# Memory keys of a decoder layer: the 512-column matmuls of a tile first, the 256-column ones behind them, and the weight rests held behind the addition that frees the bank

## The chip, the cores and the metric

The kernel runs on one core of a Trainium2 chip. The metric is the device time of one execution in microseconds (us). Before the change it is 844.3 us, the median of 3 runs (843.54 to 844.47). The profile and the trace come from one more execution of the same kernel, which took 844.19 us.

## The reference, cut to what matters

One decoder layer is computed: a mixer (stick-breaking attention and a short convolution), a cross-attention into 256 memory tokens, a SwiGLU block and a last norm. The change touches one product of the cross-attention, the memory keys.

```python
def memory_cross_attention(h, m, w_q, w_kv, w_o):
    q = (h @ w_q).reshape(b, s, MEM_HEADS, MEM_HEAD_DIM)
    kv = (m @ w_kv).reshape(b, mlen, 2, MEM_HEADS, MEM_HEAD_DIM)
    k, v = kv[:, :, 0], kv[:, :, 1]
    scores = jnp.einsum('bshd,bmhd->bhsm', q.astype(jnp.float32), k.astype(jnp.float32))
```

Here m is the normed memory, 256 x 1024, and the keys k are m times the first 1024 columns of w_kv.

## The kernel before

All products are made in fp32r in pieces: an f32 operand is split into a rounded part (hi) and the rest that the rounding left (lo), and hi x hi, hi x lo and lo x hi are added up. Weights come in tiles of 128 x 1024 through `load_w` (lines 139 to 153): SyncE starts a DMA into `wr`, ScalarE rounds it into `wh` (line 151, "the cast"), and VectorE subtracts to get `wl` (line 152, "the weight rest"). Each of `wr`, `wh` and `wl` has four buffers, so a load, a cast and a rest can run up to four tiles ahead of the matmuls that read them, and a buffer is free again when the matmuls of four tiles before are through.

The memory is held transposed, in 8 blocks of 128 of the 1024 features. For each block k, `mgs[k]` holds 512 columns: 256 memory tokens rounded (that is `mg[k][0]`) and 256 rests. The keys are made in 8 output tiles m of 128 key columns (lines 656 to 676). For one tile, the loop over k issues two matmuls each: one with `wh` over all 512 columns of `mgs[k]` (line 661), which gives hi x hi in the left half of the bank and hi x lo in the right half, and one with `wl` over the 256 rounded columns (line 663), which adds lo x hi to the left half. Then

```python
        t = tmp("km", MEM)
        nc.scalar.copy(t, ps[:, MEM:])
        nc.vector.tensor_tensor(out=t, in0=ps[:, :MEM], in1=t, op=ALU.add)
        nc.vector.tensor_tensor(out=t, in0=t, in1=rmb, op=ALU.mult)
```

ScalarE copies the right half out (line 666, "the copy"), VectorE adds the left half to it (line 667, "the addition", the last reader of the bank), multiplies by the tokens' norm factor (line 668) and, after ScalarE's rounding of the result (line 672), subtracts for the key's own rest (line 673). The banks come from a pool of two (`pmm`), so the first matmul of tile m waits for the addition of tile m-2.

Ahead of the keys stands the loop over the 8 tiles of the merged branches (`br`); behind them stand the memory values, 8 weight tiles with 12 matmuls of 512 columns each (`vm`, lines 677 to 690). The order of the instructions on each engine in this part is set by the scheduler of the framework, from the order in the code, the dependencies, and extra order-only dependencies that `after(i, earlier)` adds (line 107): i is then placed behind the instructions in `earlier`. `lows` (line 104) collects the weight rests of all `load_w` calls.

Of the kernel before, what the change touches and what calls it, by code (L numbers as in the profile page):

```python
# [11 lines left out]
ALU = mybir.AluOpType  # L12
# [4 lines left out]
KD = D // P  # L17
# [4 lines left out]
MEM = 256  # L22
# [22 lines left out]
def hybrid_layer(ctx: ExitStack, tc: tile.TileContext, xT_d, memT_d, mem_d, cols_d, wv_d, win_d,  # L45
                 wbr_d, wmix_d, wmq_d, wmk_d, wmv_d, wmo_d, wfi_d, wfo_d, gfin_d, out):
    nc = tc.nc
# [16 lines left out]
    def nm(s):  # L64
        count[0] += 1
        return f"{s}{count[0]}"

    def unit(s, cols=512):
        return upool.tile([P, cols], F32R, tag="u", name=nm(s), padded_shape=[P, 512])

    def tmp(s, cols=512):
        return tpool.tile([P, cols], F32, tag="t", name=nm(s), padded_shape=[P, 512])

    def f(ap):
        return ap.bitcast(F32)

    def mmtile(s, pool=None, tag="mm"):
        return (pool or pmm).tile([P, 512], F32, tag=tag, name=nm(s))

    def ztile(s):  # L80
        return mmtile(s, pz, "z")
# [22 lines left out]
    exps, casts, lead, lows, loads = [], [], [], [], []  # L104
    HALVES = slice(0, HD), slice(HD, P)

    def after(i, earlier):
        for e in earlier:
            tc.add_manual_dep(i.ins, e.ins.name, mybir.DependencyInfo(
                mybir.DependencyClass.NoSync, mybir.DependencyReason.DATA), reason="order")  # L110
# [23 lines left out]
    def chained(i):  # L134

        after(i, chain[-1:])
        chain.append(i)

    def load_w(src, cols=P):

        k = D // cols
        raw = wpool.tile([P, D], F32, tag="wr", name=nm("wr"))
        i = nc.sync.dma_start(raw, src)
        loads.append(i)
        if count[1] < FIRST:
            count[1] += 1
            chained(i)
        hi = wpool.tile([P, k, cols], F32R, tag="wh", name=nm("wh"))
        lo = wpool.tile([P, k, cols], F32R, tag="wl", name=nm("wl"))
        h2, l2 = (t.rearrange("p k c -> p (k c)") for t in (hi, lo))  # L150
        after(nc.scalar.copy(h2, raw), lead[-1:])  # L151
        lows.append(nc.vector.tensor_tensor(out=l2, in0=raw, in1=f(h2), op=ALU.subtract))  # L152
        return hi, lo

    def mm3(ps, a, b, start, stop, **kw):
        nc.tensor.matmul(ps, a[0], b[0], start=start, stop=False, **kw)  # L156
        nc.tensor.matmul(ps, a[0], b[1], start=False, stop=False, **kw)  # L157
        nc.tensor.matmul(ps, a[1], b[0], start=False, stop=stop, **kw)  # L158
# [11 lines left out]
    def split(src, s, scale=None, cols=512, last=()):  # L170

        hi, lo = unit(s + "h", cols), unit(s + "l", cols)
        if scale is None:
            casts.append(nc.scalar.copy(hi, src))
            after(casts[-1], last)
            nc.vector.tensor_tensor(out=lo, in0=src, in1=f(hi), op=ALU.subtract)
        else:
            nc.scalar.activation(hi, src, AF.Copy, scale=scale)
            nc.vector.scalar_tensor_tensor(out=lo, in0=src, scalar=scale, in1=f(hi),
                                           op0=ALU.mult, op1=ALU.subtract)  # L180
        return hi, lo
# [449 lines left out]
    for m in range(KD):  # L631
        sig = []
        for j in range(2):
            if (m, j) not in gates:
                gate(m, j)
            t = gates.pop((m, j))
# [4 lines left out]
        for j in (1, 0):  # L641
            if m == 0 and j == 0:
                gate(EARLY, 0)
            ps = mmtile("br")
# [8 lines left out]
            mem_split(m)  # L653


    km = []
    for m in range(KD):
        w = load_w(wmk_d[m])
        ps = mmtile("km")
        for k in range(KD):  # L660
            nc.tensor.matmul(ps, w[0][:, k, :], mgs[k], start=k == 0, stop=False,
                             skip_group_check=True)
            nc.tensor.matmul(ps[:, :MEM], w[1][:, k, :], mg[k][0], start=False, stop=k == KD - 1,
                             skip_group_check=True)
        t = tmp("km", MEM)
        nc.scalar.copy(t, ps[:, MEM:])
        nc.vector.tensor_tensor(out=t, in0=ps[:, :MEM], in1=t, op=ALU.add)
        nc.vector.tensor_tensor(out=t, in0=t, in1=rmb, op=ALU.mult)
        if m % 2 == 0:
            pair = unit("kmh"), unit("kml")  # L670
        hi, lo = (u[:, (m % 2) * MEM:(m % 2 + 1) * MEM] for u in pair)
        nc.scalar.copy(hi, t)
        nc.vector.tensor_tensor(out=lo, in0=t, in1=f(hi), op=ALU.subtract)
        km.append((hi, lo))
        if m == 0:
            merged.append(split(sig[0], "m"))
    vm = [[None] * 2 for _ in range(MT)]
    for n in range(2):
        pss = [ztile("vm") for _ in range(MT)]
        for c in range(4):  # L680
            w = load_w(wmv_d[n, c], 512)
            for j in range(2):
                k = 2 * c + j
                for t in range(MT):
                    sl = slice(t * P, (t + 1) * P)
                    mm3(pss[t], (mg[k][0][:, sl], mg[k][1][:, sl]),
                        (w[0][:, j, :], w[1][:, j, :]), k == 0, k == KD - 1)
        for t in range(MT):
            vm[t][n] = split(pss[t], "vm", rm[:, t:t + 1])
# [81 lines left out]
    for h in range(MH):  # L771
        q = q_next
        scs = []
        for t2 in range(2):
            ps = ztile("sc")
            scs.append(ps)
            for i in range(2):
                t = 2 * t2 + i
# [5 lines left out]
        for t2 in range(2):  # L784
            ps = scs[t2]
# [5 lines left out]
                                           in1=r1s[:, 2 * t2:2 * t2 + 2], op0=ALU.mult,  # L791
# [3 lines left out]
            for i in range(2):  # L795
                t = 2 * t2 + i
# [5 lines left out]
            for i in range(2):  # L802
                nc.vector.tensor_scalar(out=pr[:, i * MEM:(i + 1) * MEM],
                                        in0=pr[:, i * MEM:(i + 1) * MEM],
# [5 lines left out]
        for t in range(TT):  # L810
            for m in range(MT):
                c = (t % 2) * MEM + m * P
                nc.tensor.transpose(pt[m][:, t * P:(t + 1) * P], prs[t // 2][:, c:c + P], ident)
        ptr = [split(pt[m], "pt") for m in range(MT)]
        for j in range(2):
            ps = ztile("om")
            c = h * 256 + j * P
# [261 lines left out]
    with tc.manual_schedule(engines={mybir.EngineType.PE, mybir.EngineType.Activation,  # L1079
# [97 lines left out]
        for j in range(2, NJ - 2):  # L1177
# [6 lines left out]
            if NJ - 2 - LIGHT <= j + 1 < NJ - 2 + 1:  # L1184
                n = j + 1 - (NJ - 2 - LIGHT)
# [273 lines left out]
```

## Time and profile before

| what | value |
|---|---|
| time of the runs shown, median (lowest, highest) | 844.3 us (843.54, 844.47) |
| the profiled execution's own time | 844.19 us |
| its span | 842.4 us |
| TensorE busy / VectorE / ScalarE / GpSimd | 833.8 / 658.7 / 464.2 / 155.6 us |
| stretch of the memory keys, first key matmul to first of the values proper | 300.39 to 324.19 us |

The span is the time from the first to the last instruction of the profiled execution; 1.8 us of its time lie outside. A row of the timeline has the start and the duration in us, the engine, the line, the operation and its tiles. Matmuls are pipelined: the duration of one is from its start to its modelled end, and the next one starts before that, so what a matmul costs TensorE is the step from its start to the next start, not its duration. PE is TensorE's matmuls, PEld its weight loads, ACT ScalarE, DVE VectorE, POOL GpSimd and SP SyncE.

### The profile page before, as it was taken

How to read it: one execution, taken by the hardware profiler on the slowest of the kernel's cores; microseconds unless marked ns; L12 is line 12 of the kernel's file. 1: busy time of each engine (PE TensorE's matmuls, PEld its weight loads, DVE VectorE, ACT ScalarE, POOL GpSimd, SP SyncE). 2: the span in 40 equal slices, each digit the busy share in tenths (PEclk: the TensorE clock that was granted, in tenths of full speed). 3: DMA queues.
4: the chain of work that ended last, by engine and by line, in shares of the span. 5: the costliest groups of instructions: out<-in, count | busy, mean ns of one | idle time of the engine just before them, and what ended most of it. 6: DMA issues, size and time to landing. Idle time of an engine off the chain costs nothing.

```text
span 842.4 us, 12559 instructions
## 1 busy us (share of the span) xinstructions
PE 833.8 (99%) x4694; PEld 731.0 (87%) x4694; DVE 658.7 (78%) x1066; ACT 464.2 (55%) x835; POOL 155.6 (18%) x165
## 2 busy tenths in 40 slices
PE   9999999999999999999999999999999999999996
PEld 7888888888888888888888889999999999988885
DVE  7879899986756577586555679888887888899886
ACT  7567878674332255433444557655555555666654
POOL 0011131210666620173000101111111110000401
PEclk9999999999999999999999999999999999999998
DMA  8452454134687865566431425777677772465552
GB/s 301 151 168 102 120 115 114 59 116 172 244 308 269 315 231 189 187 230 238 134 80 51 113 51 153 198 184 190 178 181 194 189 181 85 150 224 202 176 186 101
DMA packets 51359, 143.73 MB, mean 171 GB/s; under 512 B 5761, under 2 KB 7041, under 8 KB 48482
## 3 DMA queue, kind: packets, MB, share of 16 engines
q1 hardware_dynamic: 41650, 107.89, 38.5%
q0 software_dynamic: 9360, 34.75, 15.8%
q8 instruction: 37, 0.61, 0.3%
q10 hardware_dynamic: 288, 0.28, 0.1%
q14 instruction: 24, 0.20, 0.1%
HBM read 125.20 MB, written 13.64 MB: 165 GB/s over the span
## 4 chain that ended last, share of the span: by engine, by line
PE 98%; DMA 1%; DVE 0%; ACT 0%; issue 0%; SPq 0%; DVEq 0%
PE z L883 15%; PE p L1152 12%; PE pr L156 8%; PE pr L157 8%; PE pr L158 8%; PE y L883 8%; PE v L883 4%; PE r L157 3%; PE r L156 3%; PE r L158 3%; PE v L284 2%; PE mq L157 2%; PE mq L158 2%; PE mq L156 2%; PE br L157 2%; PE br L156 2%
## 5 line engine op out<-in xcount | busy, mean ns | idle before, releaser
L151 ACT CAST wh<-wr 128x1024 fp32r<-128x1024 f32 x84 | 88.1, 1051 | 149.4 <-issue 83.7
L152 DVE TENSOR_TENSOR wl<-wr,wh 128x1024 fp32r<-128x1024 f32 x84 | 112.2, 1336 | 37.2 <-ACT wh L151 37.2
L156 PE MATMUL pr<-xgh,wh 128*128 128x512 f32 x288 | 112.8, 392 | 0.0
L157 PE MATMUL pr<-xgl,wh 128*128 128x512 f32 x288 | 112.3, 390 | 0.0
L158 PE MATMUL pr<-xgh,wl 128*128 128x512 f32 x288 | 112.2, 390 | 0.0
L607 POOL TENSOR_TENSOR pre<-pre 128x512 f32<-128x512 f32 x44 | 70.1, 1597 | 32.6 <-DMA pre<-in_w_ffn_out_dram 30.3
L852 POOL DMA_DIRECT2D ws<-in_w_ffn_in_dram x22 | 26.6, 1210 | 256.2 <-DVE wf L873 123.5
L883 PE MATMUL z<-xdh,wf 128*128 128x256 f32 x352 | 70.4, 283 | 0.0
L158 PEld LDWEIGHTS pr<-xgh,wl 128*128 128x128 f32 x288 | 54.1, 188 | 11.6
L156 PEld LDWEIGHTS pr<-xgh,wh 128*128 128x128 f32 x288 | 54.1, 188 | 10.6
L157 PEld LDWEIGHTS pr<-xgl,wh 128*128 128x128 f32 x288 | 54.1, 188 | 10.3
L904 ACT COPY sa<-z 128x256 f32<-128x256 f32 x44 | 16.4, 372 | 81.5 <-PE z L883 81.5
L883 PEld LDWEIGHTS z<-xdh,wf 128*128 128x128 f32 x352 | 58.0, 192 | 0.0
L873 DVE TENSOR_TENSOR wf<-s,wf 128x512 fp32r<-128x512 f32 x44 | 30.4, 690 | 25.7 <-ACT wf L872 25.3
L883 PE MATMUL z<-xdl,wf 128*128 128x256 f32 x176 | 49.8, 283 | 0.0
L964 DVE TENSOR_TENSOR wl<-wr,wh 128x1024 fp32r<-128x1024 f32 x33 | 41.0, 1242 | 4.3 <-ACT wh L1031 4.3
L1031 ACT CAST wh<-wr 128x1024 fp32r<-128x1024 f32 x33 | 34.6, 1050 | 4.4 <-DMA wr<-sums 2.1
L883 PE MATMUL y<-xch,wf 128*128 128x256 f32 x176 | 35.4, 283 | 0.0
L883 PE MATMUL v<-xoh,wf 128*128 128x256 f32 x176 | 35.4, 283 | 0.0
L883 PE MATMUL z<-xf,wf 128*128 128x256 f32 x264 | 35.4, 283 | 0.0
L883 PE MATMUL z<-xch,wf 128*128 128x256 f32 x176 | 35.3, 283 | 0.0
L883 PE MATMUL y<-xoh,wf 128*128 128x256 f32 x176 | 35.3, 283 | 0.0
(350 smaller groups left out, 2377.5 us busy)
## 6 DMA issues: line engine op xcount, KB each, us to landing
wr<-in_w_in_dram SPq DMA_DIRECT2D x36, 512.0 KB, 3.3
pre<-in_w_ffn_out_dram POOLq DMA_DIRECT2D x11, 1024.0 KB, 7.9
sums<-pre POOLq DMA_DIRECT2D x11, 1024.0 KB, 5.1
ws<-in_w_ffn_in_dram SPq DMA_DIRECT2D x22, 512.0 KB, 3.7
wg<-in_w_ffn_in_dram SPq DMA_DIRECT2D x22, 512.0 KB, 4.5
ws<-in_w_ffn_in_dram POOLq DMA_DIRECT2D x22, 512.0 KB, 6.1
wr<-sums SPq DMA_DIRECT2D x22, 512.0 KB, 3.9
wr<-in_w_ffn_out_dram SPq DMA_DIRECT2D x16, 512.0 KB, 3.9
```

The lines of the kernel that those rows point to most:

```text
L151: after(nc.scalar.copy(h2, raw), lead[-1:])
L152: lows.append(nc.vector.tensor_tensor(out=l2, in0=raw, in1=f(h2), op=ALU.subtract))
L156: nc.tensor.matmul(ps, a[0], b[0], start=start, stop=False, **kw)
L157: nc.tensor.matmul(ps, a[0], b[1], start=False, stop=False, **kw)
L158: nc.tensor.matmul(ps, a[1], b[0], start=False, stop=stop, **kw)
L607: nc.gpsimd.tensor_tensor(out=t[:, a, :], in0=t[:, a, :], in1=t[:, b, :], op=ALU.add)
L852: nc.gpsimd.dma_start(s13, a[:, 0:4:3, :], accum_op=ALU.add)
L873: nc.vector.tensor_tensor(out=w[:, 1, :], in0=raw, in1=f(w[:, 0, :]), op=ALU.subtract)
L883: nc.tensor.matmul(ps[:, :HS], a, b, start=i < 3 and k == 0 and j == 0, stop=k == KP - 1 and j == 2, skip_group_check=True)
L964: nc.vector.tensor_tensor(out=lo, in0=src, in1=f(hi), op=ALU.subtract)
L1031: nc.scalar.copy(hi, raw)
L1152: nc.tensor.matmul(res[i][s2], a[:, ts], b, start=j == 0 and n == 0, stop=n == 2 and j == (BEHIND - 1 if (i, s2) == (5, 1) else NJ - 1))
```

## The change

Three things change. In a key tile, the loop over k is split in two: first the 8 matmuls of 512 columns with `wh`, then the 8 of 256 columns with `wl`. The additions of the 8 tiles are collected in `ready`. And a weight rest is ordered behind an addition: that of key tile m behind the addition of tile m-4 (for m above 3), and those of the first four tiles of the memory values behind the additions of key tiles 4 to 7.

```diff
-    km = []
+    km, ready = [], []
     for m in range(KD):
         w = load_w(wmk_d[m])
+        after(lows[-1], ready[m - 4:m - 3] if m > 3 else ())
         ps = mmtile("km")
         for k in range(KD):
             nc.tensor.matmul(ps, w[0][:, k, :], mgs[k], start=k == 0, stop=False,
                              skip_group_check=True)
+        for k in range(KD):
             nc.tensor.matmul(ps[:, :MEM], w[1][:, k, :], mg[k][0], start=False, stop=k == KD - 1,
                              skip_group_check=True)
         t = tmp("km", MEM)
         nc.scalar.copy(t, ps[:, MEM:])
-        nc.vector.tensor_tensor(out=t, in0=ps[:, :MEM], in1=t, op=ALU.add)
+        ready.append(nc.vector.tensor_tensor(out=t, in0=ps[:, :MEM], in1=t, op=ALU.add))
...
         for c in range(4):
             w = load_w(wmv_d[n, c], 512)
+            if n == 0:
+                after(lows[-1], ready[c + 4:c + 5])
```

TensorE's order changes in every key tile. The rows are those at the end of key tile 1 (bank `km_2964`, weights `wh_2960` and `wl_2961`) and the start of tile 2 (bank `km_2993`). Before, TensorE has:

```order
L661 MATMUL km_2964<-mg_2378,wh_2960 128x512
L663 MATMUL km_2964<-mg_2378,wl_2961 128x256
L661 MATMUL km_2964<-mg_2381,wh_2960 128x512
L663 MATMUL km_2964<-mg_2381,wl_2961 128x256
L661 MATMUL km_2964<-mg_2493,wh_2960 128x512
L663 MATMUL km_2964<-mg_2493,wl_2961 128x256
L661 MATMUL km_2964<-mg_2496,wh_2960 128x512
L663 MATMUL km_2964<-mg_2496,wl_2961 128x256
L661 MATMUL km_2993<-mg_2181,wh_2989 128x512
```

With the change, TensorE has at the same place:

```order
L662 MATMUL km_2964<-mg_2493,wh_2960 128x512
L662 MATMUL km_2964<-mg_2496,wh_2960 128x512
L665 MATMUL km_2964<-mg_2181,wl_2961 128x256
L665 MATMUL km_2964<-mg_2184,wl_2961 128x256
L665 MATMUL km_2964<-mg_2296,wl_2961 128x256
L665 MATMUL km_2964<-mg_2299,wl_2961 128x256
L665 MATMUL km_2964<-mg_2378,wl_2961 128x256
L665 MATMUL km_2964<-mg_2381,wl_2961 128x256
L665 MATMUL km_2964<-mg_2493,wl_2961 128x256
L665 MATMUL km_2964<-mg_2496,wl_2961 128x256
L662 MATMUL km_2993<-mg_2181,wh_2989 128x512
```

The last reader of `wh_2960` stands 8 matmuls ahead of the tile's end now, where it stood one ahead. One matmul of the values (`vm_3167` with `wh_3171`), which stood between key tiles 5 and 6, stands behind tile 7 now.

VectorE's order changes around each addition. In this piece of the difference the names `km_2946` and `km_2981` are the results of key tiles 0 and 1, `kml_2951` their own rests, and `wl_3021`, `wl_3050` and `wl_3081` the weight rests of key tiles 3, 4 and 5; the rows with + are those of the change.

```order
 L152 TENSOR_TENSOR wl_3021<-wr_3018,wh_3020 128x1024
+L669 TENSOR_TENSOR km_2946<-km_2929,km_2946 128x256
 L152 TENSOR_TENSOR wl_3050<-wr_3047,wh_3049 128x1024
-L667 TENSOR_TENSOR km_2946<-km_2929,km_2946 128x256
-L668 TENSOR_TENSOR km_2946<-km_2946,rmb 128x256
+L670 TENSOR_TENSOR km_2946<-km_2946,rmb 128x256
+L675 TENSOR_TENSOR kml_2951<-km_2946,kmh_2950 128x256
+L669 TENSOR_TENSOR km_2981<-km_2964,km_2981 128x256
 L152 TENSOR_TENSOR wl_3081<-wr_3078,wh_3080 128x1024
-L673 TENSOR_TENSOR kml_2951<-km_2946,kmh_2950 128x256
-L667 TENSOR_TENSOR km_2981<-km_2964,km_2981 128x256
 L176 TENSOR_TENSOR ml_2955<-g_2851,mh_2954 128x512
```

The addition of tile 1 (lines 667 and 669) stood behind the weight rest of tile 5 and stands ahead of it now; so it is with the other tiles. ScalarE keeps its order but for one cast (`wh_3253`) that stands one place later, and SyncE and GpSimd keep theirs.

## The prediction

> **What bounds the kernel now.** The page comes first, for the engine that fills the span.
>
> ```profile
> span 842.4 us, 12559 instructions
> PE 833.8 (99%) x4694; PEld 731.0 (87%) x4694; DVE 658.7 (78%) x1066; ACT 464.2 (55%) x835; POOL 155.6 (18%) x165
> ```
>
> TensorE is busy for 99% of the span, so the time can only fall where its matmuls come closer together. The profiled execution took 844.19 us, 1.8 us more than its span and 0.1 us less than the median of the runs shown (844.3). Busy time hides short waits here, since a matmul's record is longer than its step. So I read next the timeline of TensorE in the stage of the keys, by the starts.
>
> ```profile
> 297.67 0.39 PE L156 MATMUL br<-oh,wh 128*128 128x512 f32 x1
> ...
> 300.39 0.39 PE L661 MATMUL km<-mg,wh 128*128 128x512 f32 x1
> 300.62 0.28 PE L663 MATMUL km<-mg,wl 128*128 128x256 f32 x1
> 300.73 0.40 PE L661 MATMUL km<-mg,wh 128*128 128x512 f32 x1
> ...
> 303.20 0.40 PE L661 MATMUL km<-mg,wh 128*128 128x512 f32 x1
> ...
> 305.68 0.40 PE L661 MATMUL km<-mg,wh 128*128 128x512 f32 x1
> 305.92 0.28 PE L663 MATMUL km<-mg,wl 128*128 128x256 f32 x1
> 306.03 0.49 PE L661 MATMUL km<-mg,wh 128*128 128x512 f32 x1
> 306.36 0.28 PE L663 MATMUL km<-mg,wl 128*128 128x256 f32 x1
> ...
> 308.79 0.28 PE L663 MATMUL km<-mg,wl 128*128 128x256 f32 x1
> 309.19 0.50 PE L661 MATMUL km<-mg,wh 128*128 128x512 f32 x1
> 309.53 0.27 PE L663 MATMUL km<-mg,wl 128*128 128x256 f32 x1
> ...
> 318.15 0.40 PE L156 MATMUL vm<-wh,mg 128*128 128x512 f32 x1
> 318.38 0.40 PE L661 MATMUL km<-mg,wh 128*128 128x512 f32 x1
> ...
> 324.19 0.39 PE L157 MATMUL vm<-wl,mg 128*128 128x512 f32 x1
> ```
>
> From 297.67 to 300.39 twelve matmuls of 512 columns start, 0.2267 us each: that is the step where nothing waits. The key tiles then take from 300.39 to 324.19, 23.80 us, of which 0.23 belong to the one matmul of the values at 318.15; 23.57 us are the keys' own. The first tile takes 2.81 us (300.39 to 303.20), 0.351 for a pair of a long and a short matmul. At the start of tile 3 the short matmul at 308.79 is followed only after 0.40 us, and the next long one takes a step of 0.34 (309.19 to 309.53). At the start of tile 2 it is 0.33 (306.03 to 306.36). The chain of waits, for the same stretch, says who came late.
>
> ```profile
> 306.16 1.06 ACT wh L151
> 307.25 1.22 DVE wl L152
> 308.47 0.34 DVE kml L673
> 308.81 0.35 DVE km L667
> 309.19 0.50 PE km L661
> ```
>
> Tile 3 needs the bank of tile 1. Tile 1's last long matmul ends at 306.08 (305.68 + 0.40); 0.08 later ScalarE casts the weights of tile 5, VectorE makes their rest, then the rest of key tile 0, and only then the addition that frees the bank. That is 3.1 us from matmul to matmul, where TensorE has one short matmul and one tile to fill it. The view of waits puts the sum at 1.1 us in three waits; the others are spread over long first steps.
>
> ```profile
> PEld km L661 <- DVE km L667: 1.1, 3, 0.4
> ```
>
> **The change part by part.** It adds and removes no instruction; it moves matmuls, rests and additions.
>
> *The long matmuls first.* The stage has 64 steps of 512 columns and 64 of 256. The long step is 0.2267 us, from above. For the short step in a row of its like the feed-forward stage has a row of the chain:
>
> ```profile
> 680.63 4.32 PE z L883 x36
> ```
>
> 36 matmuls of 256 columns in 4.32 us are 0.120 us each. In the key stage itself a short one between two long ones has a step of 0.11 (300.62 to 300.73), and its weight load lasts 0.188:
>
> ```profile
> L663 PEld LDWEIGHTS km<-mg,wl x64: 187/188/190, 300.4 to 323.8; 128*128 128x128 f32 x64
> ```
>
> So the short step is unknown between 0.11 and 0.188; I take 0.120, since the 36 have the same shape, fp32r and a new weight each. A tile is then 8 x (0.2267 + 0.120) = 2.773 us, and eight are 22.19 us if nothing waits. Against the 0.351 of a pair in the first tile, the new order saves 0.004 a pair, some 0.29 us in the stage if all tiles were like the first; the rest of the gain is the waits.
>
> *Does the bank come free in time?* This uses the durations of ScalarE and VectorE:
>
> ```profile
> 307.12 0.40 ACT L672 CAST kmh<-km 128x256 fp32r<-128x256 f32 x1
> 307.42 0.37 ACT L666 COPY km<-km 128x256 f32<-128x256 f32 x1
> ```
>
> ```profile
> 304.41 1.23 DVE L152 TENSOR_TENSOR wl<-wr,wh 128x1024 fp32r<-128x1024 f32 x1 [1.27 <-ACT wh L151]
> 305.56 0.42 DVE L667 TENSOR_TENSOR km<-km,km 128x256 f32<-128x256 f32 x1
> 306.01 0.42 DVE L668 TENSOR_TENSOR km<-km,rmb 128x256 f32<-128x256 f32 x1
> ```
>
> Tile 0 starts at 300.39; its last long matmul starts 7 x 0.2267 later and ends 0.40 after that, at 302.4. With 0.08 for a handoff the cast of tile 4's weights runs from 302.5 to 303.5, and it no longer stands in the copy's way: the tile's last short matmul starts at 303.04 and ends at 303.32. The copy runs from 303.4 (a ScalarE instruction starts about 0.1 before the one ahead of it ends: 307.12 + 0.40 against 307.42) to 303.8, the addition from 303.9 to 304.3. Tile 2 wants the bank at 300.39 + 2 x 2.773 = 305.94, 1.6 us later.
>
> From then on VectorE's order is a ring: addition, weight rest, multiply, (ScalarE's rounding), key rest, next addition. Its steps: 0.34 (as the chain's 0.34 from the key rest to the next instruction), 1.15 (304.41 to 305.56), 0.42, 0.08, 0.40, 0.08, 0.34, together 2.81 us, 0.04 more than a tile. The addition settles about 1.1 us behind the tile's end and frees the bank at 1.5; TensorE wants it 2.77 behind that end. The slack of 1.25 us takes six tiles with 0.04 of lag each (0.24) five times over. So the waits go entirely: I count zero where the stage had some 1.1.
>
> *The rests held back.* What is queued behind a held rest on VectorE is the multiply, and behind that ScalarE's rounding and the next addition: the ring above. Who waits for the rest is TensorE at the short matmuls of that tile, three tiles and eight long matmuls after the addition (3 x 2.77 + 1.8 - 1.5 = 8.6 us; the rest needs 1.2). The rest also frees its raw buffer, and SyncE then starts the load four tiles on:
>
> ```profile
> wr<-in_w_mem_v_dram SPq DMA_DIRECT2D x8, 512.0 KB, 3.3
> ```
>
> A rest that ends 2.7 us behind tile m's end has its successor landed at about 6.0; the cast of that one can start when tile m+4's last long matmul is through, at 4 x 2.773 - 0.7 = 10.4. So 4.4 us of cover stand over it. Its cost is zero, and only if a landing took over 7 us would the cast, and then the matmuls, be late. The moved matmul of the values costs the same 0.23 at its new place. Bounds of both: not below zero, since nothing reads a rest earlier than before; above, the waits of 1.1 us would stay.
>
> *The sum.* 23.57 - 22.19 = 1.38 us less in the key stage. Everything behind hangs on TensorE (or on what TensorE has released), so it shifts as a whole: 844.19 - 1.38 = 842.8 us.
>
> **The rivals.**
>
> *Short matmuls in a row come cheaper.* Had each the 0.11 that it has between long ones (0.113 by half the width, as 0.227 is for the full one), a tile would take 8 x (0.2267 + 0.113) = 2.72, the stage 21.74, the gain 1.83: 842.4 us. For it: the key stage shows such steps. Against it: 36 in a row of the feed-forward stage. The Trainium skill, in TensorE: Matmul & The Clock Gate, section Back-to-back issue gap, goes further: N/2.4 + 2.5 ns, an estimate of 109 and 216 ns here, which would make the stage 20.8 us and the time 841.4 us. The trace does not agree with it: 0.2267 and 0.120 stand in the rows above.
>
> *Given back later.* TensorE reaches a later place earlier and waits there for something that did not move. Against it: the loads have microseconds of cover, and ScalarE and VectorE follow TensorE's matmuls. For it: less slack shows in no row. If half of it goes, 843.5 us.
>
> *The waits are not the bank's,* and the change does not do what it says: then a first matmul of a tile waits for its weights as before, and the time stays at 844.2. Against it: the addition of tile 0 ends at 305.98 (305.56 + 0.42) and tile 2 starts at 306.03.
>
> *Slower: weight loads come to the surface.* Before, each short matmul's neighbours are long and hide a load of 0.188. In the new order eight short ones stand together. If there the load sets the step, 64 x (0.188 - 0.120) = 4.35 us come in, 2.97 net: 847.2 us. It decides from a step of 0.142 on, where 64 x 0.022 eat the 1.38. Against it stand the loads of the feed-forward stage, a group of the page with the mean in ns behind the comma.
>
> ```profile
> L883 PEld LDWEIGHTS z<-xdh,wf 128*128 128x128 f32 x352 | 58.0, 192 | 0.0
> ```
>
> They last as long, 0.192, and the 36 matmuls in a row stepped at 0.120 over them. The same page, Part 3, The mechanism, has a rule for it: a load overlaps a running matmul only in other row groups, which would put whole loads on the path. The feed-forward row speaks against that too.
>
> **How the numbers follow.** About 0.2% (1.7 us) is what a measurement of this kernel can tell from no change. The forecast of 842.8 us has a chance of 0.66; it is a gain of 0.16%, so it counts as within 0.2%, but the runs shown differ by 0.9 us among themselves, and in one case of five I expect it to be measured beyond the 0.2% (0.13). Cheaper short matmuls have 0.08, given back later 0.16, the waits not the bank's 0.05, the loads 0.05. That makes 0.21 for faster (0.13 + 0.08), 0.05 for slower and 0.74 for the rest. The range goes from 841.9, the cheaper short matmuls less half of the runs' spread of 0.9, to 844.2, the waits unchanged; the loads stay outside.
>
> **What would show it.** In the profile of the changed kernel: the first key matmul to the first of the values in 22.2 us; steps of 0.227 and 0.120 throughout; no step at a tile's start over 0.25; no wait of a key weight load for the addition; in the chain, no ScalarE or VectorE piece in this stage; the additions starting about 0.5 to 1.1 us behind the end of their tile. A short step over 0.14, waits at other tile starts, or a stage behind the keys that grew by over 0.5 us would make the prediction wrong.

## The result, and the profile after

The changed kernel takes 842.63 us (median of 22 runs, 842.03 to 843.34), the kernel before 843.97 us (22 runs, 843.21 to 844.67): 1.34 us less, a ratio of 0.9985 with a 95% interval of 0.9979 to 0.9991. The interval leaves out 1, so the change makes the kernel faster, by less than the 0.2% that the prediction took for the least that can be told; with 22 runs of each kernel 0.15% can be told as well.

The stage of the keys shows where that comes from. The timeline of TensorE in the changed kernel, at the start and at the end of the stage (a row with x8 is eight matmuls in a row, its duration reaching to the modelled end of the last):

```profile
300.92 1.98 PE L662 MATMUL km<-mg,wh 128*128 128x512 f32 x8
302.74 1.12 PE L665 MATMUL km<-mg,wl 128*128 128x256 f32 x8
303.69 2.00 PE L662 MATMUL km<-mg,wh 128*128 128x512 f32 x8
305.53 1.12 PE L665 MATMUL km<-mg,wl 128*128 128x256 f32 x8
306.48 2.00 PE L662 MATMUL km<-mg,wh 128*128 128x512 f32 x8
...
309.27 2.00 PE L662 MATMUL km<-mg,wh 128*128 128x512 f32 x8
...
312.07 2.00 PE L662 MATMUL km<-mg,wh 128*128 128x512 f32 x8
...
322.29 1.12 PE L665 MATMUL km<-mg,wl 128*128 128x256 f32 x8
323.24 0.40 PE L156 MATMUL vm<-wh,mg 128*128 128x512 f32 x1
```

From 300.92 to 323.24 are 22.32 us, where the keys had 23.56 before (23.57 from the rounded rows of the prediction): 1.24 us less. The first tile takes 2.77 us (300.92 to 303.69), every other 2.79. The chain of waits of the changed kernel in this stage names TensorE and no other engine:

```profile
303.85 1.84 PE km L662 x8
305.69 0.95 PE km L665 x8
306.64 1.84 PE km L662 x8
```

Where before the cast, the weight rest, the key rest and the addition stood in it, there is nothing left but matmuls. The timeline of VectorE shows how far ahead the addition (line 669) is now:

```profile
307.50 0.42 DVE L669 TENSOR_TENSOR km<-km,km 128x256 f32<-128x256 f32 x1
...
313.09 0.42 DVE L669 TENSOR_TENSOR km<-km,km 128x256 f32<-128x256 f32 x1
313.42 1.22 DVE L152 TENSOR_TENSOR wl<-wr,wh 128x1024 fp32r<-128x1024 f32 x1
```

Tile 1 ends at 306.48, its addition ends at 307.92, and TensorE wants the bank for tile 3 at 309.27: 1.35 us to spare. The addition at 313.09 starts 1.02 behind the end of its tile, tile 3 (312.07), and the held weight rest follows it.

The two profiled executions differ by less than the stage: spans of 842.4 and 841.5, times of 844.19 and 843.24 us. The first key matmul starts at 300.92 in the changed kernel and at 300.39 before, though nothing was changed ahead of it, and another 0.2 us went where TensorE had waited at 394 us. Two experiments below (the kernel before once more, and without the last sums) take up both.

### The profile page after: what moved, and what is told of

It is laid out like the page before. It is cut to its first block, busy times and chain, and to the rows that moved or that the text cites. A ratio compares the mean times of both kernels' runs of the same rounds, so it can differ in the third digit from the quotient of the medians.

```text
span 841.5 us, 12550 instructions
## 1 busy us (share of the span) xinstructions
PE 833.3 (99%) x4694; PEld 732.2 (87%) x4694; DVE 659.9 (78%) x1066; ACT 464.7 (55%) x835; POOL 157.6 (19%) x165
## 4 chain that ended last, share of the span: by engine, by line
PE 99%; DVE 0%; ACT 0%; DVEq 0%; issue 0%
PE z L887 15%; PE p L1156 12%; PE pr L156 8%; PE pr L158 8%; PE pr L157 8%; PE y L887 8%; PE v L887 4%; PE r L157 3%; PE r L158 3%; PE r L156 3%; PE v L284 3%; PE km L662 2%; PE mq L158 2%; PE mq L157 2%; PE mq L156 2%; PE br L156 2%
## 5 line engine op out<-in xcount | busy, mean ns | idle before, releaser
L607 POOL TENSOR_TENSOR pre<-pre 128x512 f32<-128x512 f32 x44 | 71.8, 1636 | 31.4 <-DMA pre<-in_w_ffn_out_dram 29.1
```

The source lines that it names most:

```text
L607: nc.gpsimd.tensor_tensor(out=t[:, a, :], in0=t[:, a, :], in1=t[:, b, :], op=ALU.add)
```

## The experiments

All stage lengths are from the first key matmul to the first of the row of value matmuls, less the step of a value matmul in between where there is one.

**The first part alone.** The changed kernel without its two `after` calls:

```diff
-        after(lows[-1], ready[m - 4:m - 3] if m > 3 else ())
...
-            if n == 0:
-                after(lows[-1], ready[c + 4:c + 5])
```

> Only the first part of the change: the 512-column matmuls of a key tile first, those of 256 behind; no weight rest is held, so VectorE keeps the order of before (weight rest, key rest, addition). The theory (the bank's addition comes late because the chain from the tile's last long matmul over cast, weight rest and key rest takes 3.1 us, and TensorE has 2.9 for it): the last long matmul now ends about 0.9 us earlier, the addition ends about 2.3 us behind the tile's end where TensorE wants it at 2.77, so no wait is left: the stage from the first key matmul to the first of the values takes 22.3 us as with the whole change (22.32), 842.6 +- 0.4 us or 1.3 us less than before. Rival (the hold is what takes the waits away): the waits of 1.1 us stay, the stage takes 23.3 us.

Measured: 842.39 us against 843.90 us for before, ratio 0.9982 (0.9973 to 0.9990). The rows of TensorE at both ends of the stage, and of VectorE's addition of tile 1:

```profile
300.87 1.98 PE L661 MATMUL km<-mg,wh 128*128 128x512 f32 x8
...
309.22 2.00 PE L661 MATMUL km<-mg,wh 128*128 128x512 f32 x8
...
323.19 0.40 PE L156 MATMUL vm<-wh,mg 128*128 128x512 f32 x1
```

```profile
306.80 1.23 DVE L152 TENSOR_TENSOR wl<-wr,wh 128x1024 fp32r<-128x1024 f32 x1 [0.77 <-ACT wh L151]
307.94 0.42 DVE L674 TENSOR_TENSOR kml<-km,kmh 128x256 fp32r<-128x256 f32 x1
308.28 0.42 DVE L668 TENSOR_TENSOR km<-km,km 128x256 f32<-128x256 f32 x1
```

The stage takes 22.32 us, the same as with the whole change. VectorE still makes the weight rest and the key rest ahead of the addition, but the addition ends at 308.70, 0.52 us before tile 3 wants the bank at 309.22. The hold adds slack (1.35 in place of 0.52) and no time.

**The second part alone.** Long and short matmuls alternate again, the rests are held:

```diff
-        for k in range(KD):
             nc.tensor.matmul(ps[:, :MEM], w[1][:, k, :], mg[k][0], start=False, stop=k == KD - 1,
                              skip_group_check=True)
```

> Only the second part: long and short matmuls alternate as before, and the weight rests are held behind the additions. The theory: the chain loses the weight rest (1.2 us), the addition ends about 2.0 us behind the tile's end, so no wait is left; pairs of long and short ones cost 0.347 to 0.353, eight tiles 22.2 to 22.6 us. Rival one (the runs of equal matmuls are what gains): the stage stays near 23.5 us. Rival two (only both parts together take the waits away): 22.9 us or more.

Measured: 842.89 us, ratio 0.9989 (0.9980 to 0.9998). TensorE:

```profile
299.86 0.39 PE L662 MATMUL km<-mg,wh 128*128 128x512 f32 x1
...
322.46 0.40 PE L156 MATMUL vm<-wh,mg 128*128 128x512 f32 x1
```

The stage takes 22.60 us: every wait is gone by the hold as well (no step is over 0.25 us), and a pair of a long and a short matmul costs 0.353. So either part removes the waits; the rival that only both together do it falls.

**Four banks.** The kernel before with one line changed:

```diff
-        ps = mmtile("km")
+        ps = (mmtile, otile)[m // 2 % 2]("km")
```

> The kernel before with one edit: the key tiles take their banks two by two from two pools of two, so a bank is wanted again only by the fourth tile behind. Orders on ScalarE and VectorE as before. The theory that the waits are the bank's: all waits go though rests and matmuls stand as they did, 22.2 to 22.6 us for the stage (64 pairs of 0.347 to 0.353). Rival (a first matmul waits for its weights, not for the bank): the waits stay, 23.5 us.

Measured: 842.94 us, ratio 0.9988 (0.9979 to 0.9997). The end of tile 2 and the start of tile 3, the stage's ends around them, and VectorE's addition of tile 1:

```profile
300.73 0.39 PE L661 MATMUL km<-mg,wh 128*128 128x512 f32 x1
...
309.07 0.28 PE L663 MATMUL km<-mg,wl 128*128 128x256 f32 x1
309.19 0.40 PE L661 MATMUL km<-mg,wh 128*128 128x512 f32 x1
...
323.32 0.40 PE L156 MATMUL vm<-wh,mg 128*128 128x512 f32 x1
```

```profile
309.06 0.42 DVE L667 TENSOR_TENSOR km<-km,km 128x256 f32<-128x256 f32 x1
```

TensorE starts tile 3 at 309.19, in step, while the addition of tile 1 runs until 309.48. Orders and durations on VectorE and ScalarE are those of before; only the bank's return no longer counts. The stage takes 22.60 us (rounded rows: 22.59). That shows that the waits are the bank's, and what they cost: 23.56 - 22.60 = 0.96 us against the first profile of the kernel before, and 1.03 and 1.06 us against the two later ones with its order (23.63 and 23.66, below).

**Two short matmuls behind the last long one.** The kernel before, its short matmuls one place later, VectorE's order unchanged (the added lines of the loop):

```diff
+        for n in range(KD + 1):
+            if n < KD:
+                nc.tensor.matmul(ps, w[0][:, n, :], mgs[n], start=n == 0, stop=False,
+                                 skip_group_check=True)
+            k = n - 1
+            if k >= 0:
+                nc.tensor.matmul(ps[:, :MEM], w[1][:, k, :], mg[k][0], start=False,
+                                 stop=k == KD - 1, skip_group_check=True)
```

> The kernel before with its short matmuls one place later: long 0, long 1, short 0, long 2, short 1 and so on, so that two short ones stand behind the tile's last long one, not one; VectorE's order is that of before. The theory: every wait for a bank gets shorter by one short step, 0.12 us, and none is gone where it was 0.18 to 0.29 (tiles 3 and 5): the stage falls from 23.6 to 22.9 to 23.2 us. Rival (what gains is that equal matmuls stand together): at most one eighth of the gain, 23.4 us or more.

One execution took 843.31 us; the stage runs from 299.95 to 323.48 with one value matmul in it, 23.29 us. The rows at the starts of tiles 3, 5 and 7 (each time the last two short matmuls of the tile ahead, then the first two long ones):

```profile
308.15 0.40 PE L666 MATMUL km<-mg,wl 128*128 128x256 f32 x2
308.62 0.73 PE L662 MATMUL km<-mg,wh 128*128 128x512 f32 x2
...
314.15 0.40 PE L666 MATMUL km<-mg,wl 128*128 128x256 f32 x2
314.58 0.73 PE L662 MATMUL km<-mg,wh 128*128 128x512 f32 x2
...
320.30 0.39 PE L666 MATMUL km<-mg,wl 128*128 128x256 f32 x2
320.55 0.74 PE L662 MATMUL km<-mg,wh 128*128 128x512 f32 x2
```

The wait at a tile's start is the time from the last short matmul ahead of it, less its step of 0.12:

| wait, us | tile 3 | tile 4 | tile 5 | tile 7 | stage |
|---|---|---|---|---|---|
| kernel before, first profile | 0.28 | 0.08 | 0.18 | 0.14 | 23.56 |
| kernel before once more (below) | 0.28 | 0.02 | 0.28 | 0.13 | 23.66 |
| two short matmuls behind | 0.23 | none | 0.20 | 0.01 | 23.29 |

The long first step of tile 2, 0.33 us in both profiles of the kernel before, is 0.23 here. So the stage fell by 0.27 to 0.37 us, more than the rival allows, but it stays 0.1 us above the 23.2 that I expected at most. Against the second profile every wait is shorter, by 0.02 to 0.12 us; against the first the one at tile 5 is not. The waits differ between two executions of the same kernel, and TensorE comes earlier to a tile where it has waited less at the ones ahead, so the dose can't be read from a single tile. Why the sum fell short stays open.

**Runs of four.** The changed kernel with a tile in four runs (the added lines):

```diff
+        for k0 in (0, 4):
+            for k in range(k0, k0 + 4):
+                nc.tensor.matmul(ps, w[0][:, k, :], mgs[k], start=k == 0, stop=False,
+                                 skip_group_check=True)
+            for k in range(k0, k0 + 4):
+                nc.tensor.matmul(ps[:, :MEM], w[1][:, k, :], mg[k][0], start=False,
+                                 stop=k == KD - 1, skip_group_check=True)
```

> The changed kernel (rests held) with a key tile in four runs, not two: 4 long, 4 short, 4 long, 4 short matmuls. No wait for a bank is expected (the last long matmul ends 0.5 us ahead of the tile's end and the rest is held). What is asked is why the stage took 22.32 us where 64 steps of 0.2267 and 64 of 0.120 make 22.19, and 22.60 where long and short ones alternate. Theory: each return from short to long matmuls has a price, as long steps of 0.233 and 0.236 behind a run of short ones show; 16 returns in place of 8 make it 22.4 to 22.5 us. Rival: the price is that of the short matmuls, wherever they stand: 22.32 us again.

One execution took 842.61 us, with a stage of 22.43 us:

```profile
300.01 1.07 PE L663 MATMUL km<-mg,wh 128*128 128x512 f32 x4
300.92 0.64 PE L666 MATMUL km<-mg,wl 128*128 128x256 f32 x4
301.39 1.09 PE L663 MATMUL km<-mg,wh 128*128 128x512 f32 x4
302.32 0.63 PE L666 MATMUL km<-mg,wl 128*128 128x256 f32 x4
...
322.44 0.40 PE L156 MATMUL vm<-wh,mg 128*128 128x512 f32 x1
```

The first four long ones take 0.91 (300.01 to 300.92), the next four, behind short ones, 0.93 (301.39 to 302.32). Twice the runs cost 0.11 us more in the stage.

**Two tiles at a time.** No hold, four banks, a pair's long matmuls first (the added lines, cut at the dots):

```diff
+    for m0 in range(0, KD, 2):
+        ws, banks2 = [load_w(wmk_d[m0 + i]) for i in range(2)], []
+        for w in ws:
+            ps = (mmtile, otile)[m0 // 2 % 2]("km")
+            banks2.append(ps)
...
+        for w, ps in zip(ws, banks2):
+            for k in range(KD):
+                nc.tensor.matmul(ps[:, :MEM], w[1][:, k, :], mg[k][0], start=False,
+                                 stop=k == KD - 1, skip_group_check=True)
```

> The long-first order without a hold, over two key tiles at a time: 8 long matmuls of tile m, 8 of tile m+1, then the 8 short ones of each; four banks from two pools, since a pair needs two at once. Theory of a price for each return to long matmuls: 4 returns in place of 8, 22.24 to 22.27 us for the stage, and no wait; the time 842.5 +- 0.4 us, which no measurement can tell from the changed kernel. Rival (price of the short matmuls): 22.32 us.

Measured: 842.42 us against 843.91, ratio 0.9985 (0.9975 to 0.9995), and the shortest stage of all, 22.24 us:

```profile
300.27 3.79 PE L663 MATMUL km<-mg,wh 128*128 128x512 f32 x16
303.90 2.08 PE L667 MATMUL km<-mg,wl 128*128 128x256 f32 x16
305.81 3.82 PE L663 MATMUL km<-mg,wh 128*128 128x512 f32 x16
...
322.51 0.40 PE L156 MATMUL vm<-wh,mg 128*128 128x512 f32 x1
```

By its time it cannot be told from the changed kernel, nor from the first part alone.

**The kernel before once more.**

> The kernel before once more, for a second profile. Asked is whether what its first profile shows besides the key stage comes back: the two long steps at 394.03 and 394.35 us (0.32 and 0.335 where 0.227 is the rule, 0.2 us lost), and the start of the first key matmul, which lay between 298.5 and 299.6 us behind the first matmul in six profiles. If they belong to the kernel they come back; theory: the start varies from execution to execution whatever the kernel, and the stage of the keys takes 23.5 to 23.6 us again.

One execution took 844.42 us:

```profile
300.75 0.39 PE L661 MATMUL km<-mg,wh 128*128 128x512 f32 x1
...
318.56 0.40 PE L156 MATMUL vm<-wh,mg 128*128 128x512 f32 x1
...
324.65 0.40 PE L157 MATMUL vm<-wl,mg 128*128 128x512 f32 x1
```

The first key matmul starts at 300.75, and the stage takes 23.66 us, 0.1 more than in the first profile: so far two executions of one kernel differ. There is no long step at 394: GpSimd's last sums ended at 390.57 here.

**Without the last sums.** The kernel before, one group of additions left out:

```diff
-            for a, b in ((0, 2), (2, 1), (1, 0), (3, 1)):
+            for a, b in ((0, 2), (2, 1), (1, 0), (3, 1)) if j < NJ - 1 else ():
```

> The kernel before without the four GpSimd additions of the last group of the down-projection's weight sums (their part of the output is left out); its loads and its store stay. In the first profile of before these ran from 387.48 to 393.75 us, VectorE's weight rest beside them took 2.23 us in place of 1.23, and TensorE waited at 394.03. Theory: the additions slow VectorE, so the rest takes 1.22 to 1.23 us and TensorE does not wait there; the key stage stays at 23.5 to 23.6 us. Rival: VectorE is slow there for another reason, the rest takes over 1.7 us again.

One execution took 843.38 us, with a stage of 23.63 us and no long step at 394. GpSimd and VectorE in the first profile of before, and VectorE here:

```profile
387.48 6.27 POOL L607 TENSOR_TENSOR pre<-pre 128x512 f32<-128x512 f32 x4 [9.07 <-DMA pre<-in_w_ffn_out_dram]
```

```profile
390.37 2.23 DVE L152 TENSOR_TENSOR wl<-wr,wh 128x1024 fp32r<-128x1024 f32 x1 [0.21 <-ACT wh L151]
392.52 1.77 DVE L179 SCALAR_TENSOR_TENSOR xgl<-x,gcol,xgh 128x512 fp32r<-128x512 f32 x1
```

```profile
389.88 1.23 DVE L152 TENSOR_TENSOR wl<-wr,wh 128x1024 fp32r<-128x1024 f32 x1 [0.21 <-ACT wh L151]
391.02 0.75 DVE L179 SCALAR_TENSOR_TENSOR xgl<-x,gcol,xgh 128x512 fp32r<-128x512 f32 x1
```

Beside GpSimd's additions the rest takes 2.23 us and the next instruction 1.77, without them 1.23 and 0.75. GpSimd had waited for the sums' load (9.07 us in its row), and in the nine profiles in which these additions run they begin anywhere from 382.98 to 387.48 us; the latest of them is the first profile of the kernel before, the only one in which TensorE waited at that place. So those 0.2 us are an accident of one execution, not an effect of the change. The same holds for the start: the first key matmul lay anywhere from 299.83 to 300.92 us in the ten profiles, and at 300.39, 300.75 and 299.83 in the three whose key stage has the order of before. Where that spread comes from was not looked into.

## Why the prediction was right

*What bounds.* Right: TensorE, with waits for banks that the busy share hides. Four banks showed that the waits are the bank's and that they cost 0.96 us, or up to 1.06 by the later profiles, where the view of waits had said 1.1.

*The order of the matmuls.* The mechanism was right, and its size is small but real. The long step of 0.227 and the short one of 0.120 were right inside a run. What the sum missed, and the only term of it that was mis-sized, is the floor of 22.19 us: the stage took 22.32, since each return from short to long matmuls costs something. By the starts, the 64 long steps took 0.19 us more than at 0.2267 each, and the 64 short ones 0.06 us less than at 0.120, as the first of a run steps at 0.113. The returns, and what the stage takes over 22.19 all told:

| returns within the stage | stage, us | over 22.19, us | per return, us |
|---|---|---|---|
| 3 (two tiles at a time) | 22.24 | 0.05 | 0.017 |
| 7 (the change, and its first part alone) | 22.32 | 0.13 | 0.019 |
| 15 (runs of four) | 22.43 | 0.24 | 0.016 |
| 63 (alternating, no waits) | 22.60 | 0.41 | 0.007 |

The last return of each kernel, which the expectations counted in, falls into the values behind the stage.

So the gain in the stage was 1.24, not 1.38 us: 0.96 from the waits and 0.28 from fewer returns (1.31 and 1.34 in all against the later profiles with the order of before). That the 0.28 agrees with the 0.29 that the prediction worked out is luck: a pair costs 0.353 over the stage where the first tile gave 0.351, and the floor is 22.32 in place of 22.19, and the two errors of 0.1 us cancel.

*Does the bank come free in time.* Right: the additions start 1.02 us behind the tile's end in the steady part (1.1 was worked out), with 1.35 us to spare at tile 3 (1.25 was). They do not lag: four tiles on from the addition at 313.09 they are still 1.02 behind (324.26 against 323.24).

```profile
324.26 0.42 DVE L669 TENSOR_TENSOR km<-km,km 128x256 f32<-128x256 f32 x1
```

But what places them there is not VectorE's ring, as far as the rows show. The rows of ScalarE and VectorE for tile 4, whose last long matmul ends at 314.07 (312.07 + 2.00):

```profile
314.15 1.05 ACT L151 CAST wh<-wr 128x1024 fp32r<-128x1024 f32 x1 [1.17 <-issue]
315.10 0.40 ACT L674 CAST kmh<-km 128x256 fp32r<-128x256 f32 x1
```

```profile
314.56 0.42 DVE L670 TENSOR_TENSOR km<-km,rmb 128x256 f32<-128x256 f32 x1
315.54 0.43 DVE L675 TENSOR_TENSOR kml<-km,kmh 128x256 fp32r<-128x256 f32 x1 [0.56 <-ACT kmh L674]
315.88 0.42 DVE L669 TENSOR_TENSOR km<-km,km 128x256 f32<-128x256 f32 x1
```

Behind the last long matmul comes the cast, right behind that the rounding of key tile 3, for which VectorE has waited 0.56 us, then the key rest and the addition: the chain of before without the weight rest, 1.8 us from the matmul's end to the addition's start in place of 2.7 (306.08 to 308.81 in the prediction's rows). The ring's own steps add up to 2.75 us by these rows (0.33, 1.14, 0.42, 0.08 for the handoff from the multiply as in the prediction, 0.40, 0.04 and 0.34), where the prediction had 2.81; it is a little shorter than a tile of 2.79, so the lag of 0.04 us a tile does not appear.

*The rests held back.* Right that it costs nothing. The prediction did not say that it also brings nothing on top of the first part, which the first part alone shows; without the first part it takes the waits away too.

*The sum.* 842.8 us was predicted and 842.63 measured, a gain of 1.38 us against 1.34. That the two gains are so close is in part luck. The stage gave 1.24 between the first two profiles, and the remaining 0.1 us is as much as the stage of before differs between executions; the base of the sum, 844.19, is 0.2 us above the median of 22 runs, about what TensorE lost at 394 in that one execution. The prediction was right to give most of its chance to a change within 0.2%: it is 0.15%.

*The rivals.* Cheaper short matmuls: the steps inside a run are 0.120, eight of them 0.95 with the first at 0.113. The rule of the Trainium skill that was weighed there (TensorE: Matmul & The Clock Gate, section Back-to-back issue gap, which gives it for isolated matmuls), by which the stage was estimated at 20.8 us, does not fit the 22.32 measured. The waits not the bank's: four banks took them all away. Given back later: the stretch behind the keys was not longer, some 518.2 us to the end of the span against 518.4 before (324.19 to 842.4, and 0.23 for the value matmul that stood among the keys); the difference is about the wait at 394. Weight loads at the surface: the loads of the short matmuls last 0.192 us (0.188 before) and their step is 0.120:

```profile
L665 PEld LDWEIGHTS km<-mg,wl x64: 187/192/192, 302.5 to 323.0; 128*128 128x128 f32 x64
```

## What to carry to other kernels

Where the busiest engine shows 99%, subtract starts from starts: 1.2 us of waits and small costs lay in a stage that counted as full. A wait for a bank is a race between a chain and one tile of work; here the chain missed by up to 0.3 us a tile, so any one of three edits (the last reader of the weights earlier, the addition ahead of the weight rest, two more banks) took the whole wait away, and a second one on top added only slack against it. For changes of a microsecond compare the stage, not the span: the start of the stage alone differed by 1.1 us between executions, for reasons that lay outside the change. The stage has a spread of its own, here 0.1 us, so profile the kernel before more than once.

## What the runs showed of the hardware that was not expected

A 512-column matmul behind a run of 256-column ones does not step at 0.227 at once: in the changed kernel eight long ones take 1.82 us when long ones stand ahead of them (300.92 to 302.74) and 1.84 behind short ones (303.69 to 305.53). Less what the first short step gives back, a return costs 0.016 to 0.019 us for runs of four to sixteen and 0.007 where every second matmul is short; what in TensorE makes it was not tried.

Where long and short matmuls alternate, seven pairs behind a wait took 0.347 us each (306.36 to 308.79 in the prediction's rows), against 0.353 over a stage without waits. So a part of what a wait costs comes back behind it, and the 0.96 us are less than the late steps add up to one by one (0.68 us of waits in the first row of the table above, and five long first steps, some 0.1 us over the usual each). The reason was not tried either.
